# A gated hybrid block on one core: all gate columns as four duals, two of their seven products in the head

## The chip, the core and the metric

The kernel runs on one core of a Trainium2 chip. The metric is the device time of one execution in microseconds; the time given for a kernel is the median of its runs. A core has five engines with their own instruction streams: TensorE (PE, matrix products), VectorE (DVE), ScalarE (ACT), GpSimd (POOL) and SyncE (SP, which here only issues transfers). They hand over to one another by semaphores. PSUM holds the sums of matmuls in banks of 128x512 float32.

## The reference

Sequence and width are 1024 (T and D), one layer, float32. What the change touches is the first projection and its gates:

```python
h = rms_norm(x, norm_mix_g[l]) * (1.0 + sc1) + sh1
proj = jnp.einsum('bsd,de->bse', h, w_in[l])
b_s, c_s, v_s, v_c, gl_c, gate_br = jnp.split(proj, SPLITS[:-1], axis=-1)
y_a = b_s * causal_dwconv(c_s * v_s, conv_short_w[l])
y_a = jnp.einsum('bsc,cd->bsd', y_a, w_short_out[l])
u = v_c * jax.nn.sigmoid(gl_c)
u = causal_dwconv(u, conv_conf_w[l]) + conv_conf_b[l]
...
g_a, g_b = jnp.split(jax.nn.sigmoid(gate_br), 2, axis=-1)
mix = jnp.einsum('bsd,de->bse', g_a * y_a + g_b * y_b, w_o[l])
x = x + g1 * mix
```

So h (1024 x 1024) is multiplied by 7168 columns: 56 blocks of 128, of which 16 are gates (gb0 to gb7 for the branch of the long convolution, ga0 to ga7 for the short one). A feed-forward part and a last norm follow.

## The kernel before

**Precision.** A float32 product is made of three passes in the reduced format fp32r: each operand is split into a high and a low part, and wh·xh, wh·xl, wl·xh are added in PSUM (`mm3`). A matmul of one pass is 128x128 weights by 512 columns of the sequence, which is one slot below. The sequence is two halves of 512. For weights, `split_w` casts the loaded tile `raw` to `wh` on ScalarE (L236) and takes the difference `wl` on VectorE or GpSimd (L237).

**Duals.** Most column blocks are multiplied in pairs by a Winograd-like scheme with 7 products in place of 8 ("dual"): the two halves of the inner dimension and the two halves of the sequence form a 2x2 scheme, and `PRODUCTS = "1265734"` is the order of the products. Product 1 and 2 take the plain blocks 11 and 12 of the weights and plain operands of the first half of the sequence (hT[k][0]); products 6, 5, 7, 3 take sums of the blocks (s2 = 11 + 21 + 22, s1 = 21 + 22, s3 = 11 + 21, and 12 + s2), product 4 block 22. A product is 24 matmuls: two column blocks, four blocks of k, three passes. `PAIRS` lists the two column blocks of each dual: u (long convolution's input), p and q (short one's), g (gates). Before has 13 duals, of which four are gates, scattered among the others; four gate columns, gb0 to gb3, are plain.

**Weights of a dual.** Weight units are made in a planned order (`plan`, taken by `next_w` and `fetch`, two or three ahead of TensorE). `dual_units` loads the four blocks 11, 12, 21, 22 at product 1 and makes the sums on its engine between the splits; for duals 3 and later that engine is GpSimd (rows L256, L259, L261, L303 are sums, L237 splits). `apart_units` loads each block where a product needs it: 21, 22 and 11 at product 6, 12 at product 3, 22 at product 4. There product 1 and 2 can stand far from the rest. All loads go by SP's queue into five `raw` buffers of 128x1024, used in turn; a load waits until the buffer's last reader is done, and SP issues its loads in order.

**The head.** While the modulation is worked out, `row_blocks` runs the "lead": 7 columns of weights (`w_first`, gb0 to gb2 and the four columns of the two begun duals) over the first half of the sequence, k block by k block, as these come ready. For the four dual columns it stops half way (product 1, copied out by `half_way` into m1) and goes on (to product 2). Then a second pass of the same loop takes gb0 to gb2 over the second half, with reloaded weights of 384 columns (72 matmuls), and `col_block` takes gb3 over both halves (48 matmuls). Meanwhile VectorE and ScalarE modulate the second half (x, h01 to h71: L507, L515, L516) and form the duals' operands. `gate` applies the sigmoid and stores the rows in DRAM.

**The projection.** The loop over `win_order` runs the duals' products on TensorE, each with its `product` call; `win_evac` reads the banks x, y, z of a dual after each product (copies, sums, sigmoids). Beside it the long convolution runs on VectorE, spread over the window by CONV_DUALS, and `tot` sums on GpSimd. In the last dual, `q_steps` begin what follows.

Lines behind the change are named by the numbers of before. In the changed file, L237 becomes L238, L314 (sums of `apart_units`) L315, L457/L458 L460/L461, L507 L510, L515/L516 L518/L519; L256, L259, L261, L303 become L257, L260, L262, L304.

## Time and profile before

| | us |
|---|---|
| median of 3 runs (lowest, highest) | 1457.71 (1457.65, 1459.27) |
| profiled execution, its time | 1459.06 |
| profiled execution, its span in the trace | 1457.1 |
| TensorE busy, share of the span | 1444.5, 99% |
| VectorE busy | 1183.4, 81% |
| GpSimd busy | 513.1, 35% |
| end of the lead's first pass | 60.2 |

All views are of the one profiled execution. Its span runs from the first to the last instruction; its time has 2.0 us more around it. A row of a timeline gives start and duration in us, engine, line, operation, output and inputs; what stands in brackets is the idle time of that engine before it, and the engine and tile that ended it. A row of the windows gives the stretch, its length, and for each engine the busy time and the number of instructions, then the granted clock of TensorE, the share of the DMA engines that is busy, and GB/s. Durations of consecutive instructions of an engine overlap by some 0.1 us, so their starts tell the pace. "GpSimd idle, ended by ACT wh" means that it waited for the cast of a weight tile.

### The profile page before, as it was taken

The numbers are of one execution on the slowest core, as the hardware profiler recorded it, in microseconds if no ns is written. First come the engines' busy times: TensorE is split into PE (matmuls) and PEld (weight loads), VectorE is DVE, ScalarE is ACT, GpSimd is POOL, SyncE is SP. The second block draws the span as 40 slices with busy tenths as digits, with TensorE's granted clock in tenths as the row PEclk, the third lists the DMA queues.
The fourth block names the chain that finished last, engine by engine and source line by source line (L and its number), as shares of the span: only waits on it lengthen the run. The fifth ranks groups of instructions, "written<-read, shape, count | busy, mean of one in ns | idle before, by whom it ended". The sixth has DMA issues, their size and how long they took to land.

```text
span 1457.1 us, 17725 instructions
## 1 busy us (share of the span) xinstructions
PE 1444.5 (99%) x6394; PEld 1187.3 (81%) x6394; DVE 1183.4 (81%) x1631; ACT 630.7 (43%) x914; POOL 513.1 (35%) x475
## 2 busy tenths in 40 slices
PE   8999999999999999999999999999999999999997
PEld 4888888888888888888888888888888888888887
DVE  7897999987988979989788798877876665866676
ACT  4683333333333346555236464434444443322235
POOL 0007777677677762001012001101110105662505
PEclk9999999999999999999999999999999999999999
DMA  9542122323222359666585437555554449995903
GB/s 355 203 148 92 59 101 73 116 73 101 73 87 73 122 200 328 174 215 213 194 315 183 153 101 248 206 178 184 176 179 144 142 143 355 394 372 186 358 1 116
DMA packets 90122, 259.77 MB, mean 178 GB/s; under 512 B 10241, under 2 KB 12929, under 8 KB 90034
## 3 DMA queue, kind: packets, MB, share of 16 engines
q1 hardware_dynamic: 45808, 145.18, 29.7%
q0 software_dynamic: 40192, 100.87, 21.6%
q10 hardware_dynamic: 4034, 12.59, 2.3%
q8 instruction: 50, 0.82, 0.2%
q14 instruction: 38, 0.31, 0.1%
HBM read 193.06 MB, written 65.54 MB: 177 GB/s over the span
## 4 chain that ended last, share of the span: by engine, by line
PE 97%; POOL 1%; DVE 0%; issue 0%; POOLq 0%
PE bank L426 12%; PE bank L428 12%; PE bank L425 12%; PE x L428 8%; PE x L425 8%; PE x L426 8%; PE z L425 4%; PE z L428 4%; PE z L426 4%; PE y L426 2%; PE y L428 2%; PE y L425 2%; PE mix L425 2%; PE yb L428 2%; PE yb L425 2%; PE mix L428 2%
## 5 line engine op out<-in xcount | busy, mean ns | idle before, releaser
L236 ACT CAST wh<-raw 128x1024 fp32r<-128x1024 f32 (+3 forms) x255 | 261.3, 1026 | 470.9 <-PE bank L426 146.0
L237 DVE TENSOR_TENSOR wl<-raw,wh 128x1024 fp32r<-128x1024 f32 (+3 forms) x176 | 207.4, 1179 | 60.9 <-ACT wh L236 58.3
L237 POOL TENSOR_TENSOR wl<-raw,wh 128x1024 fp32r<-128x1024 f32 x79 | 191.3, 2424 | 106.0 <-ACT wh L236 106.0
L1018 DVE SCALAR_TENSOR_TENSOR c<-diff,vec,c 128x512 f32<-128x512 f32 x232 | 168.2, 750 | 2.7
L1386 POOL DMA_DIRECT2D hid<-stage x70 | 37.3, 533 | 343.2 <-DVE stage L466 326.4
L425 PE MATMUL bank<-th,wh 128*128 128x512 f32 x312 | 121.4, 389 | 0.0
L426 PE MATMUL bank<-tl,wh 128*128 128x512 f32 x312 | 121.4, 389 | 0.0
L428 PE MATMUL bank<-th,wl 128*128 128x512 f32 x312 | 121.4, 389 | 0.0
L1018 DVE SCALAR_TENSOR_TENSOR c<-u,wsum,c 128x512 f32<-128x512 f32 x112 | 84.2, 752 | 2.3
L425 PEld LDWEIGHTS bank<-th,wh 128*128 128x128 f32 x312 | 58.6, 188 | 12.2
L426 PE MATMUL x<-tl,wh 128*128 128x512 f32 x176 | 68.5, 389 | 0.0
L425 PE MATMUL x<-th,wh 128*128 128x512 f32 x176 | 68.5, 389 | 0.0
L426 PEld LDWEIGHTS bank<-tl,wh 128*128 128x128 f32 x312 | 58.6, 188 | 12.2
L428 PEld LDWEIGHTS bank<-th,wl 128*128 128x128 f32 x312 | 58.6, 188 | 12.1
L428 PE MATMUL x<-th,wl 128*128 128x512 f32 x176 | 68.4, 390 | 0.0
L465 ACT CAST stage<-g 128x512 fp32r<-128x512 f32 x60 | 37.3, 621 | 62.6 <-DMA hid<-stage 39.7
L466 DVE TENSOR_TENSOR stage<-g,stage 128x512 fp32r<-128x512 f32 x60 | 41.2, 688 | 26.6 <-ACT stage L465 26.6
L1410 POOL DMA_DIRECT2D th<-hid x77 | 41.1, 534 | 55.4 <-PE x L428 29.0
L314 POOL TENSOR_TENSOR raw<-raw 128x1024 f32<-128x1024 f32 x8 | 20.9, 2613 | 107.9 <-DVE wl L237 103.9
L425 PE MATMUL yb<-zsh,wh 128*128 128x512 f32 x128 | 49.8, 389 | 0.0
L426 PE MATMUL yb<-zsl,wh 128*128 128x512 f32 x128 | 49.8, 389 | 0.0
L428 PE MATMUL yb<-zsh,wl 128*128 128x512 f32 x128 | 49.8, 389 | 0.0
(841 smaller groups left out, 4123.4 us busy)
## 6 DMA issues: line engine op xcount, KB each, us to landing
hid<-stage POOLq DMA_DIRECT2D x70, 512.0 KB, 4.6
raw<-in_w_duals SPq DMA_DIRECT2D x57, 512.0 KB, 3.5
raw<-in_w_fi SPq DMA_DIRECT2D x54, 512.0 KB, 4.6
th<-hid POOLq DMA_DIRECT2D x77, 256.0 KB, 5.9
tl<-hid POOLq DMA_DIRECT2D x77, 256.0 KB, 6.0
ada<-in_ada SPq DMA_DIRECT2D x24, 512.0 KB, 5.5
raw<-in_ada SPq DMA_DIRECT2D x24, 512.0 KB, 4.3
raw<-in_w_fo SPq DMA_DIRECT2D x16, 512.0 KB, 6.0
```

What stands on the lines that cost most here:

```text
L236: hi = nc.scalar.copy(wh, raw)
L237: lo = lo_engine.tensor_tensor(wl, raw, f32(wh), ALU.subtract)
L314: unit.eng.tensor_tensor(out, x, y, ALU.add)
L425: nc.tensor.matmul(ps, wh, xh, start=first, stop=False, skip_group_check=again)
L426: nc.tensor.matmul(ps, wh, xl, start=False, stop=False, skip_group_check=again)
L428: mm3.ins = nc.tensor.matmul(ps, wl, xh, start=False, stop=last, skip_group_check=again).ins
L465: t_split.act = nc.scalar.copy(hi, src).ins
L466: t_split.ins = nc.vector.tensor_tensor(lo, src, f32(hi), ALU.subtract).ins
L1018: tap.ins = nc.vector.scalar_tensor_tensor(out=out, in0=src[:, s : s + H], scalar=wt, in1=acc, op0=ALU.mult, op1=ALU.add).ins
L1386: nc.gpsimd.dma_start(hid_dram[key], s)
L1410: nc.gpsimd.dma_start(t, hid_dram[key][:, s])
```

## The change

All 16 gate columns become duals 10 to 13 (`GATED = 10`), behind the ten others. Their products 1 and 2, which need the first half of the sequence alone, are all made in the head: of three columns in the lead, which is now half way for all seven columns, and of the other five in short "streams" of 12 matmuls for product 1 and 12 for product 2 (`begin_gated`), with the weights `w_plain` and the blocks 11 and 12 of duals 12 and 13, split on VectorE. The second pass of the lead and `col_block` go, and the five reloads of `w_first` with them. Product 2 ends with the sigmoid of the gate's first half. Product 1 is copied from its bank (`part`, ScalarE), stored in DRAM by GpSimd's queue, read back by SP ahead of its dual (`begin`) and copied into the dual's bank x (`bring`, ScalarE); `win_order` leaves products 1 and 2 of duals 10 to 13 out. The weights of these duals come from `apart_units` on GpSimd instead of `dual_units`. The ring of `raw` buffers has its two pools in another order; the banks' turns, the convolution's spread and the place of `q_steps` are adapted; the splits of h00, h10, h20 move ahead of the end of the lead, and the second half's modulation is asked for in another order (`order_1`).

```diff
 PAIRS = [
-    ("u", 0), ("u", 1), ("p", 0), ("p", 1), ("u", 2), ("p", 2), ("q", 0), ("u", 3), ("p", 3), ("g", ("b", 4), ("b", 5)),
-    ("q", 2), ("u", 4), ("p", 4), ("g", ("b", 6), ("b", 7)), ("p", 5), ("u", 5), ("q", 4), ("u", 6),
-    ("p", 6), ("u", 7), ("p", 7), ("g", ("a", 0), ("a", 1)), ("q", 6), ("g", ("a", 2), ("a", 3)),
-    ("g", ("a", 4), ("a", 5)), ("g", ("a", 6), ("a", 7)),
-]
-
-
-CONV_FROM, CONV_DUALS = 1.0, 11.2
+    ("u", 0), ("u", 1), ("p", 0), ("p", 1), ("u", 2), ("p", 2), ("q", 0), ("u", 3), ("p", 3), ("u", 4),
+    ("q", 2), ("p", 4), ("p", 5), ("u", 5), ("q", 4), ("u", 6), ("p", 6), ("p", 7), ("q", 6), ("u", 7),
+] + [("g", (b, j), (b, j + 1)) for b in "ba" for j in range(0, KC, 2)]
+
+
+GATED = 10
+
+
+CONV_FROM, CONV_DUALS = 1.0, 11.06
...
-    raws = [rawp] * 3 + [rawbp] * 2
+    raws = [rawp] * 2 + [rawbp] * 2 + [rawp]
...
-    plan = [None] * KC
-    plan += [lambda: weights(w_plain[0], 1024, [modulate.ins[1]])]
     n_duals = len(PAIRS) // 2
+    plan = [lambda: weights(w_plain[0], 1024, [modulate.ins[1]])]
+    plan += [lambda d=d, b=b: weights(w_duals[d, b], 1024, [modulate.ins[1]]) for d, b in ((n_duals - 2, 0), (n_duals - 2, 1), (n_duals - 1, 0))]
     win_units = [apart_units([w_duals[d, m] for m in range(4)], nc.vector, PRODUCTS if d == 0 else "125" if d == 1 else "12",
                              (lambda: t_split.ins) if d == 1 else None) for d in range(BEGUN + 1)]
-    win_units += [dual_units([w_duals[d, m] for m in range(4)], 1024, eng=nc.gpsimd) for d in range(BEGUN + 1, n_duals)]
+    win_units += [dual_units([w_duals[d, m] for m in range(4)], 1024, eng=nc.gpsimd) for d in range(BEGUN + 1, GATED)]
+    win_units += [apart_units([w_duals[d, m] for m in range(4)], nc.gpsimd) for d in range(GATED, n_duals)]
     win_order = [(BEGUN, m) for m in "12"] + [(d, m) for d in range(BEGUN + 1) for m in PRODUCTS[2:]]
-    win_order += [(d, m) for d in range(BEGUN + 1, n_duals) for m in PRODUCTS]
+    win_order += [(d, m) for d in range(BEGUN + 1, n_duals) for m in PRODUCTS[2 * (d >= GATED) :]]
     plan += [win_units[d][m] for d, m in win_order]
+    plan.insert(5, lambda: weights(w_duals[n_duals - 1, 1], 1024, [modulate.ins[1]]))
...
+                if i > KH and k == KH:
+                    for o in range(GATES):
+                        half_way(o, outs[o])
                 xs = act(i)
                 ops.append((unit(i), xs))
             if half_way is not None and k == KH:
-                for o in range(whole, n):
-                    half_way(o - whole, outs[o])
+                for o in range(GATES, n):
...
+                for i in range(WHOLE):
+                    with tc.issue_after(modulate.ins[1]):
+                        hT[i][0] = split(x[i, 0], hl_tile, f"h{i}0")
...
-            elif kind == "g":
-                e["t"] = [uc_tile("sig", T) for _ in range(2)]
-                e["b"], e["c"] = ([t[:, s] for s in halves] for t in e["t"])
             else:
                 e["b"] = [None, g_tile("v")]
+
+        def begin():
+
+            rows = uc_tile("sig", T)
+            for i, e in enumerate(st):
+                e["t"] = uc_tile("sig", T)
+                e["b"], e["c"] = [None, rows[:, halves[i]]], [e["t"][:, s] for s in halves]
+                nc.sync.dma_start(e["c"][0], part_dram[d, i])
+
+        def bring(i):
+            nc.scalar.copy(banks["x", i], st[i]["c"][0])
...
-                elif kind == "g":
-                    nc.scalar.activation(e["b"][0], ps, AF.Sigmoid)
...
+                def store():
+                    nc.scalar.dma_start(gate_dram[j][:, halves[1]], e["b"][1])
+                    nc.scalar.dma_start(gate_dram[rest[0]], e["t"])
+                late.append(store)
...
-    plan[:KC] = [lambda k=k: weights(w_first[k][:, : GATES * P], GATES * P, [modulate.ins[0]]) for k in SECOND[KEPT:]]
...
+    part_dram, held = {}, []
+
+    def part(d, p, ps):
+
+        t = s_tile("part")
+        nc.scalar.copy(t, ps)
+        held.append((d, p, t))
+
+    def part_stores():
+
+        while held:
+            d, p, t = held.pop(0)
+            part_dram[d, p] = dram.tile([P, H], F32, name=f"part{d}{p}")
+            nc.gpsimd.dma_start(part_dram[d, p], t)
+
+    def half_way(o, ps):
         with tc.issue_after(modulate.ins[1]):
-            nc.scalar.copy(m1[i], ps)
-
-    ops = ()
-    for h in range(2):
-        lead = row_blocks(act_x if h == 0 else lambda i: act_x(SECOND[i], 1), GATES if h else LEAD, "lead", ops,
-                          again_w if h else lead_w, 1 + h, None if h else half_way, GATES)
-        if h == 0:
-            ops = [(again_w(i), xs) for i, xs in ((i, act_x(SECOND[i], 1)) for i in range(3))]
-        if h:
-            fetch(1)
-            for k in range(WHOLE):
-                with tc.issue_after(modulate.ins[2]):
-                    hT[k][0] = split(x[k, 0], hl_tile, f"h{k}0")
-            fetch(AHEAD + 1)
-        for j, ps in enumerate(lead):
-            if j < GATES:
-                with tc.issue_after(split.act) if h else ExitStack():
-                    gate("b", j, h, ps)
+            if o < GATES:
+                part(GATED + o // 2, o % 2, ps)
             else:
-                begun[(j - GATES) // 2]((j - GATES) % 2, "2", ps)
+                nc.scalar.copy(m1[o - GATES], ps)
+
+    lead = row_blocks(act_x, LEAD, "lead", (), lead_w, 1, half_way)
+    gated = [(d, p) for d in range(GATED, n_duals) for p in range(2)]
+
+    def gate_of(d, p, ps):
+        gate(*PAIRS[2 * d + p][1], 0, ps)
+
+    fetch(1)
+    for o, ps in enumerate(lead):
+        if o < GATES:
+            gate_of(*gated[o], ps)
+        else:
+            begun[(o - GATES) // 2]((o - GATES) % 2, "2", ps)
+    part_stores()
+
+    def begin_gated(m, w, streams, at=0):
+
+        for i, (d, p, ps) in enumerate(streams):
+            for k in (KH - 1, *range(KH - 1)):
+                c0 = ((i if len(streams) > 1 else at) * KH + k) * P
+                mm3([ps], slice(c0, c0 + P), w, [hT[k + at * KH][0]], m == "1" and k == KH - 1, k == KH - 2, m == "2")
+            if m == "1":
+                part(d, p, ps)
+                part_stores()
+            else:
+                gate_of(d, p, ps)
+
+    order_1 = [k + i for k in range(KH) for i in (KH, 0)]
+
+    def acts(n):
+        for _ in range(n):
+            act_x(order_1.pop(0), 1)
+
+    streams = [(d, p, (ps_tile if d < n_duals - 1 else ps2_tile)("begun")) for d, p in gated[GATES:]]
+    acts(2)
+    w = next_w()
+    begin_gated("1", w, streams[:1])
+    acts(2)
+    begin_gated("1", next_w(), streams[1:3])
+    acts(2)
+    begin_gated("2", w, streams[:1], 1)
+    acts(2)
+    begin_gated("2", next_w(), streams[1:3], 1)
...
-    for h, ps in enumerate(col_block(next_w(), hT, (0, 1), "gb")):
-        gate("b", GATES, h, ps)
-    fetch(AHEAD + 1)
+    begin_gated("1", next_w(), streams[3:])
...
+                  for d in range(BEGUN + 1, GATED)]
+    win_banks += [{(b, p): ring[i][p] for b, i in (("x", (d + 1 - GATED) % 2), ("z", 2)) for p in range(2)}
+                  for d in range(GATED, n_duals)]
     win_evacs = begun + [win_evac(d, PAIRS[2 * d : 2 * d + 2], win_banks[d]) for d in range(BEGUN, n_duals)]
     for d, m in win_order:
-        if d == n_duals - 1 and m == PRODUCTS[0]:
+        if (d, m) == (n_duals - 2, PRODUCTS[-2]):
             q_steps.pop(0)()
+        if d + 1 >= GATED and d + 1 < n_duals:
+            if m == PRODUCTS[-3]:
+                win_evacs[d + 1].begin()
+            elif m == PRODUCTS[-1]:
+                for p in range(2):
+                    win_evacs[d + 1].bring(p)
         if d + 1 < BEGUN and m == PRODUCTS[-1]:
             for p in range(2):
                 nc.scalar.copy(win_banks[d + 1]["x", p], m1[2 * (d + 1) + p])
@@ -1087,11 +1145,12 @@
             product(win_banks[d], m, th[m], win_evacs[d], onto="2")
         if (d, m) == win_order[0]:
             more_operands()
+            begin_gated("2", next_w(), streams[3:], 1)
         if (d, m) == (0, PRODUCTS[-1]):
             for h in range(2):
                 tot.append(hl_tile(f"tot{h}", dt=F32))
                 nc.gpsimd.memset(tot[h], 0.0)
-        if d == n_duals - 1:
+        if win_order.index((d, m)) >= len(win_order) - 7:
```

The first place is VectorE behind the lead's last block, h70 (the rows after h70l, the low part of the last block of the first half; rx1t and rx1r are the second half's norm, x41 and so on its blocks, wl_617 the low part of the weights of dual 12, block 11; wl_572 that of the plain column). The change has this order:

```order
L510 SCALAR_TENSOR_TENSOR x41_384<-x41_384,naff1_106,rx1r_495 128x512
L461 TENSOR_TENSOR h20l_539<-x20_283,h20h_538 128x512
L510 SCALAR_TENSOR_TENSOR x01_376<-x01_376,naff1_106,rx1r_495 128x512
L510 SCALAR_TENSOR_TENSOR x11_378<-x11_378,naff1_106,rx1r_495 128x512
L510 SCALAR_TENSOR_TENSOR x21_380<-x21_380,naff1_106,rx1r_495 128x512
L510 SCALAR_TENSOR_TENSOR x31_382<-x31_382,naff1_106,rx1r_495 128x512
L1037 TENSOR_TENSOR wsum_109<-vec_95 128x120
L519 SCALAR_TENSOR_TENSOR h41l_609<-x41_384,mod_105,h41h_608 128x512
L510 SCALAR_TENSOR_TENSOR x51_386<-x51_386,naff1_106,rx1r_495 128x512
L963 TENSOR_TENSOR x00_234<-x00_234,x01_376 128x512
L238 TENSOR_TENSOR wl_617<-raw_614,wh_616 128x1024
```

Before, at the same place (x51, h51l and so on are second-half blocks; the 128x384 tiles the reloaded weights):

```order
L507 SCALAR_TENSOR_TENSOR x71_384<-x71_384,naff1_106,rx1r_489 128x512
L516 SCALAR_TENSOR_TENSOR h61l_558<-x61_382,mod_105,h61h_557 128x512
L507 SCALAR_TENSOR_TENSOR x01_370<-x01_370,naff1_106,rx1r_489 128x512
L516 SCALAR_TENSOR_TENSOR h71l_563<-x71_384,mod_105,h71h_562 128x512
L507 SCALAR_TENSOR_TENSOR x11_372<-x11_372,naff1_106,rx1r_489 128x512
L516 SCALAR_TENSOR_TENSOR h01l_619<-x01_370,mod_105,h01h_618 128x512
L237 TENSOR_TENSOR wl_625<-raw_622,wh_624 128x384
L237 TENSOR_TENSOR wl_631<-raw_628,wh_630 128x384
L516 SCALAR_TENSOR_TENSOR h11l_645<-x11_372,mod_105,h11h_644 128x512
L237 TENSOR_TENSOR wl_651<-raw_648,wh_650 128x384
```

Six second-half modulations and a first difference now stand in one piece ahead of the split of dual 12's weights; before, each was followed by the split that the next matmuls need.

The second place is GpSimd where the weights of dual 9 end and those of dual 10 and 11 are made. Before, a dual's rows there are these (wl are splits; the first two sums are s1 and s3, the third s2, the fourth that of product 3):

```order
L256 TENSOR_TENSOR raw_3135<-raw_3127,raw_3129 128x1024
L259 TENSOR_TENSOR raw_3127<-raw_3127,raw_3123 128x1024
L237 TENSOR_TENSOR wl_3132<-raw_3123,wh_3131 128x1024
L261 TENSOR_TENSOR raw_3123<-raw_3123,raw_3135 128x1024
L237 TENSOR_TENSOR wl_3168<-raw_3125,wh_3167 128x1024
L1039 TENSOR_TENSOR tot0_1169<-tot0_1169,u5_2550 128x512
L303 TENSOR_TENSOR raw_3125<-raw_3125,raw_3123 128x1024
L1039 TENSOR_TENSOR tot1_1171<-tot1_1171,u5_2550 128x512
L237 TENSOR_TENSOR wl_3200<-raw_3123,wh_3199 128x1024
```

The change has these rows (wl_3050, wl_3081, wl_3118 are the splits of dual 9's products 7, 3, 4; raw_3148, 3150, 3152 are blocks 21, 22, 11 of dual 10, raw_3258 its block 12; raw_3155 is s2 in a buffer of its own):

```order
L238 TENSOR_TENSOR wl_3050<-raw_2902,wh_3049 128x1024
L315 TENSOR_TENSOR raw_3150<-raw_3148,raw_3150 128x1024
L238 TENSOR_TENSOR wl_3081<-raw_2900,wh_3080 128x1024
L315 TENSOR_TENSOR raw_3155<-raw_3152,raw_3150 128x1024
L315 TENSOR_TENSOR raw_3148<-raw_3148,raw_3152 128x1024
L238 TENSOR_TENSOR wl_3118<-raw_2904,wh_3117 128x1024
L238 TENSOR_TENSOR wl_3158<-raw_3155,wh_3157 128x1024
L315 TENSOR_TENSOR raw_3258<-raw_3258,raw_3155 128x1024
L238 TENSOR_TENSOR wl_3193<-raw_3150,wh_3192 128x1024
```

The sums of dual 10 now stand between the last splits of dual 9, and each reads a block loaded just ahead, not one that came with the other three.

The third place is SP's queue for the same stretch of the change (parts and q rows are other transfers in the same queue; raw_3328 and raw_3330 are blocks 21 and 22 of dual 11):

```order
L221 DMA raw_3150<-in_w_duals 128x1024
L820 DMA sig_3113<-part100_596 128x512
L820 DMA sig_3115<-part101_598 128x512
L221 DMA raw_3152<-in_w_duals 128x1024
L996 DMA q01_3688<-q0_1764 128x512
L221 DMA raw_3328<-in_w_duals 128x1024
L221 DMA raw_3258<-in_w_duals 128x1024
L996 DMA q01_3690<-q1_1766 128x512
L996 DMA q01_3692<-q2_2240 128x512
L996 DMA q01_3694<-q3_2242 128x512
L221 DMA raw_3296<-in_w_duals 128x1024
L764 DMA q6_3209<-sc6_3002 128x1024
L221 DMA raw_3330<-in_w_duals 128x1024
```

The blocks of dual 10 and dual 11 are issued one by one, each into a buffer that GpSimd has last read; before, the four blocks of a dual are issued next to each other.

More of the change, by code (lines that the diff above doesn't have):

```diff
@@ L562, in row_blocks @@
                     w, xs = ops[kk]
-                    half = half_way is not None and o >= whole
+                    half = half_way is not None
                     with tc.issue_after(first) if first else ExitStack():
@@ L747, in block_kernel @@
     act_x.sum = sum_x1
-    def again_w(i):
-        if i < KEPT:
-            return kept.pop(0)
-        return next_w(1 if i < KC - 1 else 0)
     rx_1 = None
@@ L1164, in ya_evac @@
         return evac
-    ya_banks = [{(bank, p): ring[(n_duals + n) % 3][p] for bank, n in (("x", 2 * d), ("y", 1), ("z", 1)) for p in range(2)}
+    ya_banks = [{(bank, p): ring[(1 + n) % 3][p] for bank, n in (("x", 2 * d), ("y", 1), ("z", 1)) for p in range(2)}
                 for d in range(2)]
```

29 lines of the change are left out of this document (14 added, 15 removed).

## The prediction

> **What bounds the kernel now.** I read the engine totals first, then the chain of waits, then windows of 100 us.
>
> ```profile
> span 1457.1 us, 17725 instructions
> PE 1444.5 (99%) x6394; PEld 1187.3 (81%) x6394; DVE 1183.4 (81%) x1631; ACT 630.7 (43%) x914; POOL 513.1 (35%) x475
> PE 97%; POOL 1%; DVE 0%; issue 0%; POOLq 0%
> ```
>
> TensorE is busy 99% of the span and 97% of the chain that ended last is its own matmuls. So a matmul that goes is worth its slot, and each place where TensorE has to wait is paid in full. The next view is of the input projection, where the edit works.
>
> ```profile
> 200.00:300.00 100.00, 100.00 (x443) 82.81 (x442) 94.37 (x140) 32.91 (x46) 76.66 (x35) 1.00 0.26 90
> 400.00:500.00 100.00, 100.00 (x443) 82.81 (x442) 86.85 (x121) 35.12 (x48) 76.19 (x34) 1.00 0.26 85
> 59.52 0.39 PE L425 MATMUL lead<-h70h,wh 128*128 128x512 f32 x1
> 60.20 0.39 PE L425 MATMUL lead<-h51h,wh 128*128 128x512 f32 x1
> ```
>
> TensorE has no idle moment there at a granted clock of 1.00. VectorE is at 87 to 94%, GpSimd at 76%: GpSimd's share looks comfortable, but a share says nothing of the order in which its work comes. From 59.52 to 60.20 us are three matmuls, so a slot of 128x512 is 0.68/3 = 0.2266 us. A product of a dual is 24 slots (4 row blocks of k, two rows of columns, 3 passes): 5.44 us.
>
> **What goes.** The lead of seven columns stays as long as it was. Beside it, before has 13 duals of 7 products, less products 1 and 2 of the two begun duals, which the lead holds: 87; and for the plain gate columns 72 slots in the second pass of the lead and 48 in the fourth column's block: 120. After: 14 duals, less those 4 and less products 1 and 2 of the four gate duals: 98 − 12 = 86; and five short streams of 24 slots: 120 again. The instruction order has 6327 matmul rows before, 6303 after: 24 fewer. **Term 1: −24 × 0.2266 = −5.44 us.** All else can only take from this.
>
> **The head.** The lead ends at 60.20 us. After it TensorE takes the first stream's 12 slots with the plain weights, until 62.9 us, and then needs the weights of dual 12, block 11: wh at 62.9, wl two slots on, some 63.6 with the first pass of both rows. When do these come? ScalarE and VectorE rows of before, at the same place:
>
> ```profile
> 41.08 1.06 ACT L882 COPY m<-lead 128x512 f32<-128x512 f32 x2
> 53.68 0.73 ACT L515 ACTIVATE h70h<-x,mod 128x512 fp32r<-128x512 f32 x1
> 56.09 1.28 ACT L621 ACT_TABLE_LOAD   x1
> 73.68 1.03 ACT L236 CAST wh<-raw 128x1024 fp32r<-128x1024 f32 x1
> 74.61 0.61 ACT L457 CAST h00h<-x 128x512 fp32r<-128x512 f32 x1
> 54.56 0.74 DVE L516 SCALAR_TENSOR_TENSOR h70l<-x,mod,h70h 128x512 fp32r<-128x512 f32 x1
> 55.23 0.68 DVE L495 SCALAR_TENSOR_TENSOR rx1t<-ss,rx1t 128x512 f32<-128x512 f32 x1
> 55.94 0.69 DVE L496 SCALAR_TENSOR_TENSOR rx1r<-rx1t,rx1r 128x512 f32<-128x512 f32 x1
> 56.67 1.42 DVE L507 SCALAR_TENSOR_TENSOR x<-x,naff,rx1r 128x512 f32<-128x512 f32 x2
> 72.92 0.28 DVE L987 TENSOR_TENSOR wsum<-vec 128x120 f32<-128x120 f32 x1
> 75.89 0.68 DVE L458 TENSOR_TENSOR h00l<-x,h00h 128x512 fp32r<-128x512 f32 x1
> 78.49 1.22 DVE L237 TENSOR_TENSOR wl<-raw,wh 128x1024 fp32r<-128x1024 f32 x1
> 79.62 0.69 DVE L458 TENSOR_TENSOR h20l<-x,h20h 128x512 fp32r<-128x512 f32 x1
> ```
>
> In the new VectorE order stand between the start of rx1t (55.23) and the wl of dual 12: rx1t and rx1r (0.71 each, start to start), the three low parts of h00, h10, h20 (0.61 each, rows L458 lie 0.6 us apart from their neighbours), the plain wl (78.49 to 79.62: 1.14), six modulations of the second half and h41l (7 × 0.67, from 54.56 to 55.23 and like rows), wsum (0.25) and the first difference (0.61, kin of L458). That is 1.42 + 1.83 + 1.14 + 4.69 + 0.25 + 0.61 = 9.94 us, so this wl starts at 65.2 and ends at 66.3. ScalarE's chain is no later: from 53.68, with the plain wh, three more casts of 0.61, the table load of 1.28, three gates, four copies, h41h and x01, its wh ends near 64.5.
>
> Everything here may move a little later still. In the loop of the lead, three new copies of a half-way bank (0.53 each by L882) stand ahead of the wh of the sixth block on ScalarE, and the first waits for TensorE. I put this at 0.8 us, between 0 and 1.6 (all three in the way). So wl at 66.3 to 67.9, I take 67.0, against 63.6. **Term 2: 67.0 − 63.6 = +3.4 us, between 2.7 and 4.3.** Later streams have their operands in time by the same walk. What covered it before was the second half of the plain gate columns: 72 slots with weights of only 384 columns, whose splits cost 0.5 us each, half of what these take.
>
> **GpSimd in the gate duals.** Before, each dual loads its four blocks at once and GpSimd makes the sums between splits, always ahead:
>
> ```profile
> 464.25 2.41 POOL L237 TENSOR_TENSOR wl<-raw,wh 128x1024 fp32r<-128x1024 f32 x1 [3.04 <-ACT wh L236]
> 469.68 2.39 POOL L237 TENSOR_TENSOR wl<-raw,wh 128x1024 fp32r<-128x1024 f32 x1 [3.02 <-ACT wh L236]
> 472.15 2.40 POOL L256 TENSOR_TENSOR raw<-raw 128x1024 f32<-128x1024 f32 x1
> 474.62 2.40 POOL L259 TENSOR_TENSOR raw<-raw 128x1024 f32<-128x1024 f32 x1
> 476.99 2.40 POOL L237 TENSOR_TENSOR wl<-raw,wh 128x1024 fp32r<-128x1024 f32 x1
> 479.47 2.74 POOL L261 TENSOR_TENSOR raw<-raw 128x1024 f32<-128x1024 f32 x1
> ```
>
> In the first two rows it waits 3.0 us of each 5.44 for ScalarE's wh, which itself waits for TensorE to give up a buffer: here GpSimd is not late, TensorE is. The duals 10 to 13 come by the apart way instead: product 6 asks for blocks 21, 22, 11 and a fifth, new buffer for s2, product 3 for block 12, product 4 for block 22 again. Six buffers a dual out of a ring of five, each filled when a GpSimd instruction has freed it. How long such a turn takes, from the freeing to the first sum, is shown where the early duals did just that:
>
> ```profile
> 126.97 2.40 POOL L237 TENSOR_TENSOR wl<-raw,wh 128x1024 fp32r<-128x1024 f32 x1 [3.21 <-ACT wh L236]
> 133.02 4.89 POOL L314 TENSOR_TENSOR raw<-raw 128x1024 f32<-128x1024 f32 x2 [3.65 <-issue]
> L237 POOL TENSOR_TENSOR wl<-raw,wh x15: 2397/2407/2416, 118.3 to 197.7; 128x1024 fp32r<-128x1024 f32 x15
> L314 POOL TENSOR_TENSOR raw<-raw x8: 2402/2412/3272, 106.8 to 145.1; 128x1024 f32<-128x1024 f32 x8
> DMA to landing us min/median/max: 3.4/3.5/4.5
> ```
>
> The split ended at 129.37, the sum began at 133.02: 3.65 us, of which the transfer is 3.5. A split or a sum is 2.41 us.
>
> Now the chain. By the order of SP and GpSimd and what their instructions wait for, these hang on one another in the new program, (9,7) being product 7 of dual 9: split (9,7) frees block 22 of dual 10; s1 needs it; split (9,3) behind s1 frees block 11; s2, then s3, then split (9,4), which frees block 12 of dual 10; add3; split (10,5), which frees block 22 of dual 11; s1, split (10,7), which frees block 11; s3, split (10,3), s2, which frees block 12; add3, split (10,4). Those are 15 instructions of 2.41 us, 36.2 us, and six turns of 3.65 us, 21.9 us: 58.1 us. The chain can start 1.15 us (a wh cast and its hand-over, by the row at 73.68) after TensorE ends product (9,2), which frees the buffer that split (9,7) fills. TensorE needs split (10,4) after the nine products between, 9 × 5.44 = 48.9, and two slots, 0.45. **Term 3: 1.15 + 58.1 − 49.4 = +9.8 us.** It falls in steps, by the same sum made up to each split: some 0.8 us at (9,4), 0.6 at (10,7), 3.0 at (10,3), 5.4 at (10,4). With these stalls behind it GpSimd is ahead again: five splits and four sums of a later gate dual are 9 × 2.41 = 21.7 of 27.2 us, and the loads of duals 12 and 13 are asked for from buffers that came free earlier, by 1.1 us or more at the split that I find tightest. Bounds: if the transfers land in 2.5 us, one less than the shortest seen here, the chain is 52 us and 4 remain; if a turn takes 4.65 (the 4.5 us landing above), it is +16. I take 9.8 since both durations come from the same instructions and the same load, on this queue.
>
> [...]
>
> ```profile
> 10.09 0.49 PE L630 MATMUL clock<-sq,ones 128*128 128x128 f32 x2 [1.89 <-ACT sq L577]
> 1440.00:1457.00 17.00, 8.72 (x67) 8.08 (x65) 8.22 (x18) 5.72 (x15) 11.84 (x14) 0.86 0.52 187
> ```
>
> In this trace the one early stall, 1.89 us, is too short to tell, and the last stretch, where TensorE is busy for 8.72 of 17 us, shows a clock of 0.86: a clock that falls with idleness is there, no row gives its time. The sum stands without it.
>
> **What costs nothing.** The halves of eight gate rows stored and read back (256 KB each) ride on queues whose DMA share is 0.26 here, and are due tens of products later. ScalarE's eight copies into a bank add 8 × 0.6 us over 100 us in which it is at 33 to 35%. The convolution's work on VectorE comes a little denser (its window is now 11.06 duals, the products counted fewer); at 87 to 94% busy I walked its evaluations through the new order and found none later than before by more than 1 us, with a bank's slack of a product. If that cover is gone, each product pays up to 0.5 us; this is in the range.
>
> **Sum**: −5.4 + 3.4 + 9.8 = +7.8 us. The profiled execution took 1459.06 (its span 1457.1, 2.0 us around it), which makes it 1466.9; its time is 1.35 us over the median of the runs, 1457.71, to which I refer the forecast: **1465.5 us**.
>
> **Rivals.** (B) *The ring hides its turns.* Loads may be issued sooner than I read (a freed buffer two back), so that term 3 is nil; the 3.5 us landing speaks against, the 106 us in which GpSimd idles for ScalarE over the run speaks for some slack. The head stays: 1457.7 − 5.4 + 3.4 = 1455.7. (C) *The clean gain*: the head also hidden, as VectorE's instructions may be issued in another order than by the walk; 1452.3. Against it is the 9.9 us of VectorE work between rx1t and the wl, all of it in order. This is the side opposite to my forecast; it decides where both chains end within a product's slack. (D) *The chain repeats* in each gate dual: GpSimd's nine instructions and three turns of 3.65 exposed make 32.7 us against 27.2, 5.4 us more for each of duals 12 and 13, behind the chain of term 3: 1465.5 + 10.8 = 1476. The slack that the first stalls give speaks against it.
>
> **How the numbers follow.** Forecast (head and one chain) 0.50, B 0.15, C 0.22, D 0.13. The time is the forecast's, 1465.5. Its own range is 1459 to 1472 by the bounds of terms 2 and 3 taken together. The range that holds 8 in 10 takes in half of C and part of D: 1452 to 1473. What a measurement here tells from no change is 0.2%, 2.9 us: faster means below 1454.8 and holds C and a quarter of B (0.26), slower is above 1460.6 (0.63), the rest 0.11.
>
> **What would show it.** Right: a gap of about 3 us in TensorE near 63 us, ended by VectorE's wl; four gaps ahead of (9,4), (10,7), (10,3), (10,4), near 445 to 475 us, ended by GpSimd's wl and growing; sums L315 there with idle time of some 3.6 us ahead, released by a load; 24 fewer matmuls. Wrong: TensorE at 100% in the windows from 400 to 500 us (B or C); gaps in duals 12 and 13 as well (D); idle TensorE ended by VectorE in the middle of the projection, where I see none.

## The result and the profile after

The change made the kernel slower: 1481.7 us (median of 4 runs, 1480.4 to 1482.1) against 1457.9 before, a ratio of 1.016 with a 95% interval of 1.0142 to 1.0177. The forecast was slower, at 1465.5 us with a range up to 1473: the sign holds, the size does not.

The totals and the chain of waits of the changed kernel, from its page:

```profile
span 1478.6 us, 17734 instructions
PE 1450.3 (98%) x6370; PEld 1188.8 (80%) x6370; DVE 1186.1 (80%) x1630; ACT 635.1 (43%) x922; POOL 528.0 (36%) x486
PE 87%; POOL 4%; DMA 3%; ACT 2%; DVE 1%; issue 1%; POOLq 0%; ACTq 0%; SPq 0%; DVEq 0%
```

TensorE has 24 matmul records fewer, as counted, and is nevertheless busy 5.8 us longer: some matmuls must be slower. GpSimd, 1% of the chain before, is 4% now, and transfers, which were not in it, are 3%. Next what TensorE waits for (engine, line and tile; whom it waits for; us in total, times, longest):

```profile
PE bank L431 <- POOL wl L238: 13.2, 5, 5.2
PE begun L428 <- ACT wh L237: 2.6, 1, 2.6
PE bank L431 <- DVE wl L238: 0.5, 1, 0.5
```

These are the places in its timeline, with a few rows behind each:

```profile
65.75 0.79 PE L428 MATMUL begun<-h30h,wh 128*128 128x512 f32 x1 [2.58 <-ACT wh L237]
448.11 0.50 PE L431 MATMUL bank<-th,wl 128*128 128x512 f32 x1 [0.38 <-POOL wl L238]
469.92 0.79 PE L431 MATMUL bank<-th,wl 128*128 128x512 f32 x1 [5.19 <-POOL wl L238]
470.51 0.63 PE L428 MATMUL bank<-th,wh 128*128 128x512 f32 x1
470.94 0.63 PE L429 MATMUL bank<-tl,wh 128*128 128x512 f32 x1
478.25 0.50 PE L431 MATMUL bank<-h41h,wl 128*128 128x512 f32 x1 [0.29 <-POOL wl L238]
489.04 0.80 PE L431 MATMUL bank<-th,wl 128*128 128x512 f32 x1 [5.06 <-POOL wl L238]
536.42 0.80 PE L431 MATMUL bank<-th,wl 128*128 128x512 f32 x1 [2.24 <-POOL wl L238]
594.92 0.50 PE L431 MATMUL bank<-q2h,wl 128*128 128x512 f32 x1 [0.55 <-DVE wl L238]
```

The head's stall is at 65.75, and the four at 448, 470, 478 and 489 are (9,4), (10,7), (10,3) and (10,4), the four places forecast. The one at 536 is product 7 of dual 12, where no stall was expected, and the one at 595 is behind the projection. After the stall of 5.19 us the matmuls start 0.43 us apart (470.51, 470.94) and not 0.2266: half clock. The windows show it in the granted clock, the last number but two:

```profile
65.00:70.00 5.00, 4.25 (x9) 2.96 (x10) 5.00 (x7) 5.00 (x8) 0.54 (x1) 0.52 0.24 39
470.00:475.00 5.00, 5.00 (x12) 3.92 (x13) 0.00 (x0) 0.88 (x2) 1.56 (x1) 0.52 0.61 210
```

From the starts of the matmuls, what each place takes beyond 0.2267 us a slot:

| place | wait and half clock, us | forecast |
|---|---|---|
| one product less | −5.4 | −5.4 |
| head, 63 to 72 us | 5.9 | 3.4 |
| (9,4) to (10,4), with the half clock inside | 13.9 | 9.8 |
| half clock behind (10,4) | 1.4 | 0 |
| (12,7), with half clock | 4.0 | 0 |
| split behind the projection, 595 us | 0.7 | 0 |
| sum | 20.5 | 7.8 |

The spans differ by 21.5 us; 1.0 of it is not placed. Why GpSimd is late is in its own timeline:

```profile
434.84 2.40 POOL L238 TENSOR_TENSOR wl<-raw,wh 128x1024 fp32r<-128x1024 f32 x1
440.91 4.78 POOL L315 TENSOR_TENSOR raw<-raw 128x1024 f32<-128x1024 f32 x2 [3.67 <-DMA raw<-in_w_duals]
445.65 4.75 POOL L238 TENSOR_TENSOR wl<-raw,wh 128x1024 fp32r<-128x1024 f32 x2
454.14 2.40 POOL L315 TENSOR_TENSOR raw<-raw 128x1024 f32<-128x1024 f32 x1 [3.74 <-DMA raw<-in_w_duals]
456.49 2.41 POOL L238 TENSOR_TENSOR wl<-raw,wh 128x1024 fp32r<-128x1024 f32 x1
458.85 2.57 POOL L1089 TENSOR_TENSOR tot<-tot,u 128x512 f32<-128x512 f32 x2
465.23 2.34 POOL L315 TENSOR_TENSOR raw<-raw 128x1024 f32<-128x1024 f32 x1 [3.81 <-DMA raw<-in_w_duals]
473.44 2.39 POOL L315 TENSOR_TENSOR raw<-raw 128x1024 f32<-128x1024 f32 x1 [3.58 <-DMA raw<-in_w_duals]
484.32 2.35 POOL L315 TENSOR_TENSOR raw<-raw 128x1024 f32<-128x1024 f32 x1 [3.64 <-DMA raw<-in_w_duals]
```

Split and sum alternate with a wait for a load, as forecast. Four of the turns (from the freeing of a buffer to the first sum that uses the new load) are 3.6 to 3.7 us. Two are longer: the split of (9,4) ends at 448.0 and the sum that needs its buffer starts at 454.1, 6.1 us; the split of (10,5) ends at 458.9 and s1 starts at 465.2, 6.3 us. (The bracket gives 3.8, since other work fills the rest.)

### The profile page after: what moved, and what is told of

Its sections match the earlier page's. It is cut to its first block, busy times and chain, and to the rows that moved or that the text cites. A ratio compares the mean times of both kernels' runs of the same rounds, so it can differ in the third digit from the quotient of the medians.

```text
span 1478.6 us, 17734 instructions
## 1 busy us (share of the span) xinstructions
PE 1450.3 (98%) x6370; PEld 1188.8 (80%) x6370; DVE 1186.1 (80%) x1630; ACT 635.1 (43%) x922; POOL 528.0 (36%) x486
## 4 chain that ended last, share of the span: by engine, by line
PE 87%; POOL 4%; DMA 3%; ACT 2%; DVE 1%; issue 1%; POOLq 0%; ACTq 0%; SPq 0%; DVEq 0%
PE bank L431 10%; PE bank L428 10%; PE bank L429 10%; PE x L431 8%; PE x L428 8%; PE x L429 8%; PE z L428 4%; PE z L431 4%; PE z L429 4%; PE y L428 2%; PE y L431 2%; PE y L429 2%; PE mix L429 2%; PE yb L429 2%; PE yb L431 2%; PE mix L428 2%
## 5 line engine op out<-in xcount | busy, mean ns | idle before, releaser
L237 ACT CAST wh<-raw 128x1024 fp32r<-128x1024 f32 (+2 forms) x253 | 261.8, 1037 | 456.8 <-PE bank L429 142.0
L238 DVE TENSOR_TENSOR wl<-raw,wh 128x1024 fp32r<-128x1024 f32 (+2 forms) x175 | 213.0, 1219 | 60.6 <-ACT wh L237 57.8
L431 PE MATMUL bank<-th,wl 128*128 128x512 f32 x336 | 133.6, 398 | 12.9 <-POOL wl L238 12.9
L428 PE MATMUL bank<-th,wh 128*128 128x512 f32 x336 | 132.7, 395 | 0.0
L429 PE MATMUL bank<-tl,wh 128*128 128x512 f32 x336 | 132.4, 394 | 0.0
L431 PEld LDWEIGHTS bank<-th,wl 128*128 128x128 f32 x336 | 64.4, 192 | 28.2 <-POOL wl L238 14.6
L315 POOL TENSOR_TENSOR raw<-raw 128x1024 f32<-128x1024 f32 x24 | 59.7, 2491 | 47.9 <-DMA raw<-in_w_duals 43.6
L429 PEld LDWEIGHTS bank<-tl,wh 128*128 128x128 f32 x336 | 64.2, 191 | 13.6
L428 PEld LDWEIGHTS bank<-th,wh 128*128 128x128 f32 x336 | 64.4, 192 | 13.3
```

Of the source, the lines that this page charges most:

```text
L237: hi = nc.scalar.copy(wh, raw)
L238: lo = lo_engine.tensor_tensor(wl, raw, f32(wh), ALU.subtract)
L315: unit.eng.tensor_tensor(out, x, y, ALU.add)
L428: nc.tensor.matmul(ps, wh, xh, start=first, stop=False, skip_group_check=again)
L429: nc.tensor.matmul(ps, wh, xl, start=False, stop=False, skip_group_check=again)
L431: mm3.ins = nc.tensor.matmul(ps, wl, xh, start=False, stop=last, skip_group_check=again).ins
```

## The experiments

All edits are to the changed kernel. Times are medians; the kernel before was run on the same chip beside each.

**e1, the head alone.**

```diff
-    fetch(1)
+    fetch(2)
     for o, ps in enumerate(lead):
```

> Only the head: the weights of dual 12, block 11, are asked for one unit earlier, so that their cast and split stand ahead of the lead's evacuations and the second half's modulations. Theory (a stall of 2.6 + 0.4 us near 64 us, and a stretch of half clock behind it that costs 2.7 us more because of the stall): both go, about -5.8 us, 1476 us. Rival 1 (the slow clock near 66 to 72 us comes from something else, such as the transfers there): -3.1 us, 1478.6, with matmuls still 0.43 us apart after 65 us. Rival 2 (the evacuations that now come later make TensorE wait elsewhere in the head): no gain, 1481 or more. The four stalls between 448 and 540 us stay in each case.

1476.4 us (4 runs, 1475.1 to 1479.2), ratio 1.0119 (1.0102 to 1.0136): −5.3 us. The wait at 66 us is gone and with it the half clock (mean granted clock of the profiled execution 0.994, of the changed kernel's 0.992); 0.6 us of waiting for a gate's evacuation is left. The stalls from 444 us on stay. Rival 1 falls, since both parts went.

**e2, the stall filled.** Eleven matmuls are added, whose result the next matmul overwrites.

```diff
+    for _ in range(11):
+        with tc.issue_after(mm3.ins):
+            nc.tensor.matmul(streams[1][2], w[0][:, :P], hT[KH - 1][0][0], start=True, stop=True)
     begin_gated("1", next_w(), streams[1:3])
```

> The changed kernel with 11 extra matmuls (11 x 0.2266 = 2.5 us) put between the first stream and the matmuls that wait for the weights of dual 12; their result is overwritten. The wait itself stays as it is in time: the weights come no sooner. Theory (TensorE's idleness brings the half clock): the matmuls behind 65.7 us run 0.2266 apart and not 0.43, so -2.7 us, 1479.0 us, although there is more work. Rival (the clock falls for another reason, or at a fixed place): matmuls still 0.43 apart, 1481.7 us or up to 2.5 more.

1480.9 us, but 4 runs from 1477.0 to 1482.9: inconclusive in time. The mean granted clock of the profiled execution is 0.993, against 0.992 in the changed kernel's. e12 and e13 repeat it where nothing later can hide it.

**e3, the q transfers later.**

```diff
-            nc.sync.dma_start(f32(b[i, h, k]), q_dram[k + KH * i][:, halves[h]])
+            with tc.issue_after(load.ins):
+                nc.sync.dma_start(f32(b[i, h, k]), q_dram[k + KH * i][:, halves[h]])
...
-        nc.sync.dma_start(q_dram[j], sc[j])
+        with tc.issue_after(load.ins):
+            nc.sync.dma_start(q_dram[j], sc[j])
...
+        if (d, m) == (GATED, PRODUCTS[-1]):
+            for n in range(6, 8):
+                q_store(n)
```

> The transfers of q (eight loads of 256 KB, two stores of 512 KB) that lie between 437 and 460 us in SP's queue are issued later, behind loads of weights; all else is as in the changed kernel. Theory (two of the six turns of a raw buffer took 6.1 and 6.3 us and not 3.65 because they shared the DMA engines with these transfers): the turns are 3.6 to 3.9 us, the stall of 5.2 us ahead of (10,7) falls below 1.5 us, the chain up to (10,4) is 5 us shorter: 1476 to 1477.5 us. Rival (turns are slow there for another reason, for instance that the instruction ahead on GpSimd, the two sums of tot, hold the load back): no change, 1481.7, turns still above 6 us.

1484.9 us, ratio 1.0186 (1.0169 to 1.0202): 3.2 us slower than the changed kernel, where 4 to 6 us less were expected. The stall at (10,7) fell to 2.6 us and not below 1.5. Two timelines tell why, first GpSimd, then TensorE:

```profile
452.71 2.40 POOL L315 TENSOR_TENSOR raw<-raw 128x1024 f32<-128x1024 f32 x1 [3.54 <-DMA raw<-in_w_duals]
461.34 2.39 POOL L315 TENSOR_TENSOR raw<-raw 128x1024 f32<-128x1024 f32 x1 [1.36 <-issue]
```

```profile
596.47 0.80 PE L431 MATMUL bank<-q2h,wl 128*128 128x512 f32 x1 [4.14 <-DVE wl L238]
597.06 0.63 PE L428 MATMUL bank<-q2h,wh 128*128 128x512 f32 x1
```

The turn before s1 fell from 6.3 to 3.9 us (its split ends at 457.5, s1 starts at 461.3), so that one had been sharing the DMA engines with the q transfers. The other stayed at 5.9 us (446.8 to 452.7): there two loads of weights and a store of the convolution run together. The chain up to (10,4) gained 2.4 us, and the transfers moved to where the DMA engines were full anyway: behind the projection VectorE's split is 4.1 us late, with 2.8 us of half clock behind it (granted clock 0.95 from 550 to 620 us), against a loss of 0.7 in all and a clock of 1.00 in the changed kernel.

**e4, the blocks of a gate dual together.** GpSimd's work is the same nine instructions.

```diff
+                if m == "6":
+                    for b in ("21", "22", "11", "12"):
+                        a[b] = get(b)
+                    a["s1"] = raw_tile()
...
+                return split_w(a[{"6": "11", "5": "s1", "7": "21", "3": "12", "4": "22"}[m]], 1024, (), eng)
```

> The gate duals keep their five splits and four sums on GpSimd, but all four blocks are asked for at once at product 6, block 22 is kept for product 4 and s1 gets a buffer of its own: five buffers a dual and not six, one turn ahead of the sums of a dual and not one ahead of each. Theory (the turns in series with the sums make the stalls, not GpSimd's work): at most one wait of some 2 to 4 us a dual is left, 6 to 10 us in all with the clock behind it, against 20: 1468 to 1474 us. Rival (nine instructions of 2.41 us a dual, with the sums of tot, are more than GpSimd can do in time): as the changed kernel, 1479 to 1483 us.

1470.2 us, ratio 1.0081 (1.0066 to 1.0096). Three waits for GpSimd are left, 5.9 us together, and one of 2.7 us for VectorE's split behind the projection. With the same splits and sums on GpSimd 11.5 us are gone, so the loads between them, with the half clock behind their stalls (granted clock 0.99 from 400 to 550 us, against 0.95 in the changed kernel), cost that much, and not the amount of its work.

**e5, s2 in place: five buffers a dual.**

```diff
-    win_units += [apart_units([w_duals[d, m] for m in range(4)], nc.gpsimd) for d in range(GATED, n_duals)]
+    win_units += [apart_units([w_duals[d, m] for m in range(4)], nc.gpsimd, "") for d in range(GATED, n_duals)]
```

> The gate duals make s2 in the buffer of block 11 and s3 ahead of it, as dual 2 does, so a dual takes five buffers of the ring and not six; blocks 12 and 22 are still asked for at products 3 and 4. Work on GpSimd, order of the ring and the transfers of q are those of the changed kernel. Theory (each buffer of the ring that is wanted before GpSimd is through with it puts a turn into the chain; with five a dual, each is wanted one product later): the waits at (10,7), (10,4) and in dual 12 go, 2 to 5 us of stall are left: 1463 to 1469 us. Rival (GpSimd's work): 1479 to 1483.

1463.7 us, ratio 1.0035 (1.0021 to 1.0048): −18.0 us. Of the stalls from 440 to 550 us one of 1.6 us at (10,3) is left. Each load still waits for GpSimd, but one product earlier.

**e6, the ring's order put back.**

```diff
-    raws = [rawp] * 2 + [rawbp] * 2 + [rawp]
+    raws = [rawp] * 3 + [rawbp] * 2
```

> Only the order of the two pools in the ring of raw buffers is put back to that of before. Theory: a ring of five is a ring of five; the turns keep their places within one product, and the time stays within 4 us of the changed kernel, 1478 to 1486 us. Rival (the changed order of the pools makes the turns): back by the 14 us of the stalls in duals 9 to 12, 1465 to 1470 us.

1481.4 us, ratio 1.0155 (1.014 to 1.0171): no difference. The stalls move to other products and add up to the same.

**e7, sums on VectorE; e8, with the head of e1.**

```diff
+    win_units += [apart_units([w_duals[d, m] for m in range(4)], nc.vector, "6") for d in range(GATED, n_duals)]
```

> Of the gate duals, s1, s2 and the split of product 6 are made by VectorE (1.14 us each) in place of GpSimd; six buffers a dual, as in the changed kernel. GpSimd keeps s3, the sum of product 3 and four splits. Theory (chain): the turns stay, but the instructions between them are shorter by 1.3 us each and no longer stand in one queue, so the stalls of 448 to 540 us go but for 1 or 2 us: 1460 to 1465 us. Rival (VectorE is at 83 to 94% there, and 12 instructions more make it the bound): TensorE waits for VectorE's evacuations, 1466 us or more.

> The edits of the runs e1 (weights of dual 12 asked for earlier in the head) and e7 (s1, s2 and a split of the gate duals on VectorE) together. If the head's 5.8 us and the stalls of the gate duals are all that the change lost, what is left is its gain of one product: 1457.9 - 5.4 = 1452.5 us, up to 1455 with a wait of 1 or 2 us left. Rival (there is a cost besides these two, in the transfers or after the projection): 1456 us or more.

1466.1 us (1.005, 1.0037 to 1.0064) and 1461.3 us (1.0019, 1.001 to 1.0028). GpSimd's stalls are gone, but both are above their theory and in their rival's region, e7 only just (1466.1 against 1466): VectorE is now late with the sums that free the banks. From e7's waits of TensorE:

```profile
PE bank L428 <- DVE sig L782: 3.0, 2, 2.9
PE begun L428 <- ACT wh L237: 2.6, 1, 2.6
PE bank L431 <- DVE wl L238: 2.4, 3, 1.5
```

The last row is the split behind the projection, late here too. In e5 VectorE's timeline shows what stands ahead of it:

```profile
573.57 1.23 DVE L361 TENSOR_TENSOR raw<-raw 128x1024 f32<-128x1024 f32 x1 [7.02 <-issue]
574.71 1.29 DVE L1009 TENSOR_TENSOR q5l<-q,q5h 128x512 fp32r<-128x512 f32 x2
575.92 1.22 DVE L238 TENSOR_TENSOR wl<-raw,wh 128x1024 fp32r<-128x1024 f32 x1
```

L361 is the sum s2 of the next stage's weights, which by the program needs an adding transfer (one that adds to what lies in the buffer) of GpSimd's queue. VectorE stood still 7 us ahead of it, and the split that TensorE needed stood behind it. The row names no releaser; that it was this transfer is read from the program, and e10 tests the order.

**e9, e10, e11: what beats both.** e9 joins e1 and e5 and gives VectorE one split of dual 10; e10 puts the sum L361 behind the split; e11 also turns the gates' order around.

```diff
+    win_units += [apart_units([w_duals[d, m] for m in range(4)], nc.vector, "7" if d == GATED else "") for d in range(GATED, n_duals)]
...
+                with tc.issue_after(split_w.lo):
+                    nc.vector.tensor_tensor(raw, raw, a["s1"], ALU.add)
...
-] + [("g", (b, j), (b, j + 1)) for b in "ba" for j in range(0, KC, 2)]
+] + [("g", (b, j), (b, j + 1)) for b in "ab" for j in range(0, KC, 2)]
```

> The edits of e1 (weights of dual 12 asked for earlier) and e5 (s2 in place, five buffers a dual) together, and in dual 10 alone the split of product 7 on VectorE (one instruction of 1.14 us), which takes 2.41 us out of the chain that ends in e5's last stall at (10,3), 1.6 us. Theory: e5's 1463.7 less the head (e1: 5.3 us) less that stall (1.8): 1456.6 us; what then stands above 1457.9 - 5.4 = 1452.5 are VectorE's late splits near 575 to 600 us (1.9 us and a stretch of half clock in e5). Rival (the instruction more on VectorE makes it late, as twelve did in e7 and e8): 1459 us or more, with TensorE's waits ended by VectorE's sums of the gates.

> e9, and in the stage behind the projection the sum s2 of the weights (which waits up to 7 us for an adding transfer on GpSimd's queue) is put behind the split that was asked for before it. Theory (VectorE's queue stands still at that sum, and the split that TensorE needs stands behind it): TensorE's wait near 575 to 595 us and the half clock behind it go, 2 to 3.5 us off e9: 1453 to 1455 us. Rival (the transfers themselves are late, since the DMA engines are full from 545 to 590 us, so the wait moves to the next product): as e9 within 1 us.

> e10 with the gates of the short branch (a) as duals 10 and 11, those of the long branch (b) as 12 and 13: the rows that the next stage reads come first, and the last stores are of rows needed later. Theory: VectorE's waits for the reload of the a gates (1 us twice in e5, 3.5 and 2.1 in e8) go; TensorE had slack there, so 0 to 1 us off e10. Rival (the b gates stored last collide with the next stage's loads): within 0.5 us of e10 or slower.

e9: 1458.7 us (11 runs, 1455.7 to 1459.7), ratio 0.9998 (0.9989 to 1.0007), 2 us above the theory and below its rival. No stall from 440 to 550 us is above 0.4 us; two late splits behind the projection are left, 3.4 us together. e10: 1455.7 us, 0.9984 (0.9975 to 0.9993), 3 us off e9 and 0.7 above the upper end expected. e11: 1455.9 us, 0.9981 (0.9972 to 0.999), no different from e10, as its rival said. So the change can beat the kernel before, by 0.2%, about half of its 5.4 us. What TensorE still waits for in e10, the largest past the start:

```profile
PE bank L429 <- ACT vz L1212: 0.9, 1, 0.9
PE ss L605 <- ACT sumh L598: 0.8, 1, 0.8
PE begun L429 <- ACT sig L628: 0.6, 1, 0.6
PE bank L432 <- DVE wl L238: 0.5, 1, 0.5
```

**e12 and e13, the price of the clock alone.** e10 without e1's edit, and the same with e2's filler.

> e10 without the earlier weights in the head: the one place where TensorE still stands still for long is the head. Theory (a stall of 3.0 us and a stretch of half clock of 2.7 us behind it): 5.7 us, less the 0.8 us that e10 waits there for another reason, above e10's 1455.7: 1460.5 us. Rival (the stretch of half clock costs nothing in the end, since what follows has slack to give): 1458 us.

> e12 with the 11 extra matmuls of e2 in the head's stall. Theory (idleness of 2.6 us brings the half clock; work that is thrown away keeps the full one): the weights come no sooner, but the stretch behind them runs at 0.2266 us a matmul: 2.7 us below e12, 1457.8 us. Rival (the clock falls there for another reason): as e12 within 0.5 us or slower.

e12: 1459.5 us (11 runs, 1458.5 to 1462.5), ratio 1.0009 (1.0 to 1.0018), between its theory (1460.5) and its rival (1458). e13: 1457.6 us (11 runs, 1455.5 to 1458.9), ratio 0.9989 (0.998 to 0.9998), 1.9 us below e12 where 2.7 were expected. Eleven more matmuls make the kernel faster: idleness has a price beyond its own length, 1.9 us here. It is not the same in every execution. The profiled one of e12 had the same stall of 2.58 us and full clock behind it; e12, then e13, 65 to 70 us:

```profile
65.00:70.00 5.00, 3.33 (x13) 2.47 (x14) 5.00 (x8) 5.00 (x9) 0.54 (x1) 1.00 0.25 33
```

```profile
65.00:70.00 5.00, 4.66 (x20) 3.22 (x19) 5.00 (x7) 5.00 (x9) 0.54 (x1) 1.00 0.30 50
```

The changed kernel had 0.52 in this window.

## Why the prediction was wrong

**What goes** was right: 24 matmul records fewer, 5.4 us; e10 keeps part of it in time. Rivals B (the turns hidden) and C (the clean gain) fell with the first rows of the timeline.

**Term 2, the head, 3.4 us**: the wait was right, its price was not. The first matmul with wl starts at 67.39 (forecast: wl at 67.0), and the waits make 2.9 us. The other 3.0 of the 5.9 are half clock. In e4 and e12, whose profiled executions kept the full clock there (1.00 from 65 to 70 us), the same place cost 3.8 us, near the forecast; at half clock TensorE reaches the matmul that needs wl later and waits less for it (0.2 us and not 0.7), so half clock adds 2.1 us to the sum. e1 took away 5.3 us by moving the weights alone. One detail was wrong: "ScalarE's chain is no later". It was ScalarE that TensorE waited for first.

**Term 3, the chain of turns, 9.8 us**: the mechanism was right in its links, the six turns and the four places. e4 and e5 show that it is the turns and not GpSimd's load, e6 that it is not the ring's order. The size was short by two things. "Both durations come from the same instructions and the same load, on this queue" is the step that failed here: 3.65 us was measured in an early stretch with little traffic (DMA share 0.26 from 120 to 140 us), and two of the six turns took 6.1 and 6.3 us (share 0.97 from 448.0 to 454.1 and 0.87 from 458.9 to 465.2 us). That is 5.1 us more, of which 4.1 arrived at (10,4). e3 shows for one of the two that the q transfers made it; for the other it shows that they did not; that the other loads and the store beside it did is only argued. (Its lower bound, transfers of 2.5 us, lies one below the median of its row, 3.5, and not below the shortest, 3.4; the sum does not hang on it.) And the places were right but their sizes were not: the 5.2 us at (10,7), forecast as 0.6, came from the slow turns ahead of it.

**The step that failed most is "the sum stands without it"**, the half clock set at nothing. It takes 3.0 us in the head (2.1 beyond what the shorter wait gives back), 1.4 behind (10,4) and 1.6 behind (12,7). The 2.4 us behind (10,7) should cost nothing, as the chain of weights sets the end there and the next wait is the shorter for them; that is argued, and no run takes it apart. The changed kernel's trace shows half clock behind stalls of 2.2 us (matmuls 0.43 us apart at 537 us) and 2.6 us (granted clock 0.50 from 65.21 to 72.04 us), while e12 kept 1.00 behind the same 2.6 us. The one early row of before, 1.89 us idle with a granted clock of 1.00 from 8 to 13 us, was one execution; the last section sets such stalls side by side.

**"By 1.1 us or more at the split that I find tightest"** was wrong, though the prediction does not name its split: (12,7) came 2.2 us late. Ahead of it GpSimd makes two sums for dual 13 whose blocks wait for a load (idle 1.3 us), and the two sums of tot (2.5 us): a margin of 1.1 us held by adding durations does not survive a chain that is already late (this last step is argued; no run takes it apart). That is a part of rival D, which had a chance of 0.13; e5 takes it away with the sixth buffer.

**"What costs nothing"** was wrong for the transfers. Behind the projection the DMA engines are full, from 1.01 to 1.03 of their time between 560 and 590 us, and VectorE waits there in its queue, by the program for one of them. They were as full before (1.03 and 1.02 from 560 to 580 us), where no split came late for TensorE; which transfer of the change tips it is not shown. In the changed kernel this cost 0.7 us, in e3 and e5, where the projection ends earlier or brings more transfers along, 7 and 3.7. e10 shows that the order of VectorE's queue decides, not the transfer: with the sum behind the split, 3 us went.

From 1465.5 to 1481.7 are 16.2 us: 2.5 in the head, 5.5 on the chain with the clock behind it, 4.0 at (12,7), 0.7 behind the projection, 1.0 not placed; the rest is that the profiled execution of before lay 1.2 us above its median and that of after 1.3 below.

## What to carry to other kernels

Where a weight pipeline refills its buffers one by one, count the turns (freed, issued, landed) that stand in series with the work of the engine that frees them, and take the turn's length from the traffic of that very stretch (3.65 us early in the kernel, 6.1 and 6.3 for two of the six turns here); one buffer less per group was worth 18 us here, and a busy share of 70% on that engine said nothing of it. A stall of TensorE can cost more than itself, unless what follows is waiting for something else anyway: here 1.6 us of half clock stood behind one of 2.2 us, 3.0 behind one of 2.6, and in e12 none behind the same 2.6. Where a queue is worked in order, as VectorE's was here (7.0 us still at one sum in e5), put what waits for a transfer behind what the bottleneck needs next: 3 us in e10.

## What the runs showed of the hardware

The half clock behind a stall is not certain and not of one length. The same stall of 2.58 to 2.60 us in the head was followed, in the profiled executions, by full clock in e4 and e12 (granted clock 1.00 from 65 to 70 us), by 1.4 us of loss in e3 and e6 (0.66), and by 3.0 us in the changed kernel (0.52) and e7 (0.50). Stalls of other lengths, with what stands behind them (at a granted clock of 1.00 the matmuls start 0.2266 us apart and a row of one shows 0.39 us, at 0.50 they start 0.43 us apart and it shows 0.63):

| stall, us | execution and its end, us | behind it |
|---|---|---|
| 1.89 | before, 10.09 | granted clock 1.00 from 8 to 13 us |
| 1.91 | e5, 577.19 | a matmul of 0.62 us at 577.76 |
| 2.08 | e9, 571.30 | matmuls 0.23 us apart (571.63, 571.86) |
| 2.24 | changed kernel, 536.42 | matmuls 0.43 us apart (537.01, 537.44) |
| 2.87 | e7, 504.05 | a matmul of 0.63 us at 504.60 |
| 4.14 | e3, 596.47 | a matmul of 0.63 us at 597.06 |
| 5.06 | changed kernel, 489.04 | matmuls 0.43 us apart (489.63, 490.06) |
| 5.19 | changed kernel, 469.92 | matmuls 0.43 us apart (470.51, 470.94) |

Behind the three longest the loss is 1.4 us (5.06), 2.4 (5.19) and 2.8 (4.14). In the changed kernel, up to its last matmuls, the granted clock is half from 65.21 to 72.04, 467.98 to 474.81, 488.46 to 491.88 and 536.25 to 539.66 us. Around the head's stall the windows of the changed kernel, then those of e12, read:

```profile
61.80:65.21 3.41, 1.36 (x7) 0.79 (x5) 2.85 (x6) 3.41 (x7) 0.00 (x0) 1.00 0.84 320
65.21:72.04 6.83, 6.29 (x14) 4.51 (x15) 6.83 (x10) 5.59 (x9) 0.54 (x1) 0.50 0.48 151
72.04:75.45 3.41, 3.41 (x16) 2.78 (x16) 0.77 (x2) 1.59 (x3) 0.54 (x1) 1.00 0.40 163
```

```profile
61.69:65.10 3.41, 1.72 (x8) 1.10 (x6) 2.85 (x6) 3.37 (x7) 0.00 (x0) 1.00 0.90 329
65.10:68.51 3.41, 1.84 (x7) 1.23 (x8) 3.41 (x5) 3.41 (x6) 0.54 (x1) 1.00 0.02 6
```

The stall of 2.58 us ends at 65.75 us in the first and at 65.99 in the second; the one has a granted clock of 0.50 behind it, the other 1.00. What decides between them is not shown by a run; so it is open why the head cost 3.8 us and not 5.9 in the profiled executions of e4 and e12. The 11 runs of e12 lie 3.9 us apart, with a mean granted clock of 0.998 in the fastest and 0.996 in the slowest; only one of them has a trace.
